# All sixteen modulation rows of the first feed-forward made by TensorE in four column tiles of 32

## The chip, the cores and the metric

The kernel runs on one core of one Trainium2 chip. The time is device time in microseconds (us), the median of three runs. The core has a matrix engine (TensorE, PE in the profile, whose weight loads are listed as PEld), a vector engine (VectorE, DVE), a scalar engine (ScalarE, ACT), GpSimd (POOL) and a queue engine that issues transfers (SyncE, SP). Each of them runs its own instructions in the order in which they stand.

## The reference

One layer of a streaming encoder over 1024 tokens of width 1024, in float32. A conditioning vector makes nine modulation vectors of 1024 numbers, and the first two of them (shift `sh1` and scale `sc1`) enter the input of the first feed-forward:

```python
c_act = jax.nn.silu(c)
mod = c_act @ w_mod[l] + b_mod[l]
sh1, sc1, gt1, sh2, sc2, gt2, sh3, sc3, gt3 = jnp.split(mod, N_MOD, axis=-1)
u = modulate(rmsnorm(h, ffn1_norm_g[l]), sh1, sc1)      # u * (1 + sc1) + sh1
h = h + 0.5 * gt1[:, None, :] * swiglu(u, ffn1_w_gate[l], ffn1_w_up[l], ffn1_w_down[l])
```

Latent attention beside an RWKV-7 mixer, a second feed-forward and a last norm follow; they are not touched.

## The kernel before, in words

Activations lie transposed: 128 of the 1024 features on the partitions, tokens along the free dimension, so that an activation is eight tiles d = 0..7 for each half a = 0, 1 of 512 tokens. The first feed-forward begins with `up_plain`, which makes two blocks of the hidden layer without the seven-product scheme of the later ones. For half 0, and then for half 1, it multiplies the eight input tiles by two gate and two up blocks into four accumulators; each product is three matmuls on a high and a low part (`mm3`, L66). That is 96 matmuls of 512 columns for each half, 12 for each input tile. An input tile is ready when it has been normalized (`norm_raw`, L315 to L319: even d by VectorE and ScalarE, odd d by GpSimd and ScalarE), which needs the modulation numbers of its d, and when it has been split (`split`, L59 on ScalarE, then L60 on VectorE). The first low-part matmul of a tile waits for L60.

A modulation row is 128 numbers of one vector v for one d. For the first feed-forward there are sixteen: v = 0 (shift) and v = 1 (scale), d = 0..7. Those of d = 0 and 1 are made by `mod_first` on TensorE: per row eight matmuls, each with one column of the conditioning vector as weights, into one partition of a PSUM tile; a copy by ScalarE (L155), two small matmuls that turn the rows into columns (L158), and an addition of the bias by VectorE (L161). Those of d = 2..7 are made by `mod_one` on VectorE: a product with the spread vector `cact`, summed along the free dimension (L138, with a read of the accumulator), and an addition (L141). `cact` is made by `spread_c` (L117, L118). It is also used later by `mod_steps` for the other seven vectors.

Half 1 needs the sums of squares of its tokens first (`root(1)`: squares L202 on ScalarE, additions L206 on VectorE, eight small matmuls L214, square root L252, reciprocal L253, and `spread` with L224, one matmul L228 and a copy L229). The squares (`nsq`) and the copied rows (`row`) take their room in turn from the same four slots `fs[8:]`, in the order in which the program asks for them. The PSUM tiles called `norm` take turns in banks 6 and 7.

The program is written once in this order, but the scheduler of the tile framework moves each engine's instructions by its own estimate of when they can run. What stands where in the built program is shown with the change.

Of the kernel before, what the change touches and what calls it, by code (L numbers as in the profile page):

```python
# [22 lines left out]
P = 128  # L23
D = 1024
S = 1024
HB = 512
ND = D // P
# [48 lines left out]
def ps(k, name):  # L76
    b = next(k.bank[name])
    return k.psum.tile([P, HB], F32, name="ps_" + name, tag=f"bank{b}", bufs=1)


def tmp(k, name, n=HB, dt=F32):

    pool, tag, size = next(k.spare if n == HB else k.wide)
    return pool.tile([P, size], dt, name=name, tag=tag)[:, :n]
# [44 lines left out]
def mod_loads(k, v, d):  # L129
    w = tmp(k, "wmod", D)  # L130
    k.nc.sync.dma_start(out=w, in_=k.I["w_mod"][v * ND + d])
    return w


def mod_one(k, v, d, w):

    m = k.mod[:, v, d : d + 1]
    k.nc.vector.scalar_tensor_tensor(  # L138
        out=w, in0=w, scalar=1.0, in1=k.cact, op0=ALU.mult, op1=ALU.mult, accum_out=m
    )  # L140
    k.nc.vector.tensor_tensor(out=m, in0=m, in1=k.bmod[:, v * ND + d : v * ND + d + 1], op=ALU.add)  # L141


def mod_first(k, d, w):

    nc = k.nc
    t = ps(k, "norm")
    for v in range(2):
        for i in range(ND):
            nc.tensor.matmul(  # L150
                t[0:1, v * P : (v + 1) * P], lhsT=k.ccol[:, i : i + 1], rhs=w[v][:, i * P : (i + 1) * P],
                start=i == 0, stop=i == ND - 1,
            )
    row = tmp(k, "row")[0:1, : 2 * P]
    nc.scalar.copy(out=row, in_=t[0:1, : 2 * P])  # L155
    t = ps(k, "norm")[:, :2]
    for v in range(2):
        nc.tensor.matmul(  # L158
            t[:, v : v + 1], lhsT=row[:, v * P : (v + 1) * P], rhs=k.ones[0:1, 0:1], start=True, stop=True
        )  # L160
    nc.vector.tensor_tensor(  # L161
        out=k.mod[:, :2, d], in0=t, in1=k.bmod[:, : 2 * ND].rearrange("p (v d) -> p v d", d=ND)[:, :, d], op=ALU.add
    )
# [593 lines left out]
def scratch(k, pool):  # L757
    d = lambda name, *shape: [pool.tile([P, *shape], F32, name=f"{name}{a}") for a in range(2)]
    k.hD = d("hD", ND, HB)
    k.hidD = [pool.tile([P, D], F32, name=f"hidD{i}") for i in range(NF)]  # L760
    k.sinD = d("sinD", HB)
    k.cosD = d("cosD", HB)
    k.arD = d("arD", NJ, 8, P)
    k.m3D = d("m3D", 8, 8, 2, L)
    k.akD = d("akD", 8, 4, L)
    k.vD = d("vD", 4, NJ, P)
    k.ybD = d("ybD", NJ, HB)
    k.oD = d("oD", NH, HB)
    k.boD = d("boD", NJ, HB)
    k.lgD = d("lgD", NJ, HB)  # L770
    k.xD, k.fD = (pool.tile([8 * NCH, L, L], F32, name=n) for n in ("xD", "fD"))
    k.tD = pool.tile([8 * NCH, HL, HL], F32, name="tD")
# [767 lines left out]
def setup(ctx, k, tc, I, out):  # L1540
    k.nc = nc = tc.nc
    k.tc = tc
    k.I = I
    k.out = out
    k.const = ctx.enter_context(tc.tile_pool(name="const", bufs=1, side="left"))
    k.dram = ctx.enter_context(tc.tile_pool(name="dram", bufs=1, space=DRAM))
    ct = lambda name, *shape, dt=F32: k.const.tile([P, *shape], dt, name=name)
    k.ident = ct("ident", P)
    make_identity(nc, k.ident)
    k.ones = ct("ones", P)  # L1550
    nc.gpsimd.memset(k.ones, 1.0)
    for name, value in (("eps", EPS), ("halfpi", math.pi / 2)):
        setattr(k, name, ct(name, 1))
        nc.gpsimd.memset(getattr(k, name), value)
    k.bd = ct("bd", P)
    nc.gpsimd.memset(k.bd, 0.0)
    nc.gpsimd.memset(k.bd[0:64, 0:64], 1.0)
    nc.gpsimd.memset(k.bd[64:128, 64:128], 1.0)
    k.cst = ct("cst", 2 + P)
    nc.scalar.dma_start(out=k.cst, in_=I["cst"])  # L1560
    k.wmask = k.cst[:, 2:]
    k.mod = ct("mod", 9, ND)
    k.WL = ct("WL", NJ, NCH)
    k.oss = ct("oss", 8)
    k.qs = ct("qs", 2, 8)
    k.gs = {n: ct("gs_" + n, ND) for n in ("ffn1_norm_g", "mix_norm_g", "ffn2_norm_g")}
    scratch(k, k.dram)
# [19 lines left out]
def tile_layer(ctx, tc, I, out):  # L1587
    k = Ctx()
    setup(ctx, k, tc, I, out)
    nc = k.nc  # L1590
# [10 lines left out]
    with pool_("ffn1") as pool:  # L1601
# [15 lines left out]
        early = 2  # L1617
        slices = {}

        def load_mods(ds):  # L1620
            for d in ds:
                for v in (1, 0):
                    if d < early:
                        w = slices[v, d] = tmp(k, "wmod", D)
                        nc.sync.dma_start(out=w.rearrange("p (i q) -> p i q", q=P), in_=I["w_mod_in"][v * ND + d])
                    else:
                        slices[v, d] = mod_loads(k, v, d)

        def mods(d):
            if d < early:  # L1630
                mod_first(k, d, [slices[v, d] for v in range(2)])
            else:
                for v in (1, 0):
                    mod_one(k, v, d, slices[v, d])
            gain(k, "ffn1_norm_g", 1, slice(d, d + 1))

        load_mods(range(early))
# [29 lines left out]
        x = []  # L1667
# [96 lines left out]
    with pool_("inv", "left") as ip, pool_("chain") as pool:  # L1764
# [8 lines left out]
        for p in range(NP2):  # L1773
            o = ops.pop(0)
            even, odd, norm, gate = outputs(k, pool, o)
# [46 lines left out]
    x = []  # L1822
# [101 lines left out]
```

## Time and profile before

| | |
|---|---|
| median of three runs | 2100.34 us (2097.65 to 2102.45) |
| the profiled execution | 2099.98 us, of which its span is 2098.1 us |
| TensorE busy | 2023.0 us, 96% of the span |
| VectorE busy | 1508.9 us, 72% |
| ScalarE busy | 926.8 us, 44% |
| TensorE busy in the first 100 us | 81.06 us |

The span runs from the first instruction to the last. Busy times of different engines overlap. A busy matrix engine can still be held up, since the ends of its matmuls are modelled; how many matmuls run in a stretch tells more.

### The profile page before, as it was taken

The page shows a single profiled execution, that of the slowest core. Times are in us where ns is not written, and L with a number is a line of the kernel's source. Part 1 is how long each engine was busy: PE and PEld are TensorE (multiplying, and loading weights), DVE is VectorE, ACT ScalarE, POOL GpSimd, SP SyncE. Part 2 cuts the span into 40 slices and gives each one's busy share as a digit, 9 for nine tenths or more (in the row PEclk, how much of TensorE's full clock was granted, in tenths as well). Part 3 has the DMA queues.
Part 4 walks back from the last instruction along what each step waited for, and adds up shares of the span by engine and source line. Part 5 has one row for each costly group of instructions (what it writes and reads, how often), then busy time and mean ns, then how long its engine had stood idle before and what let it go on. Part 6 is the DMA issues. An engine that isn't in the chain of part 4 may idle for free.

```text
span 2098.1 us, 28595 instructions
## 1 busy us (share of the span) xinstructions
PE 2023.0 (96%) x10624; PEld 1636.3 (78%) x10624; DVE 1508.9 (72%) x2710; ACT 926.8 (44%) x1600; POOL 232.3 (11%) x250
## 2 busy tenths in 40 slices
PE   6999999999999999898979999999999999999998
PEld 4788878887888776676868888787888888878887
DVE  6999896569996567697565666567556556599975
ACT  5643333344433466644344444455333333453433
POOL 1100000000000244332133222111000000000001
PEclk8999999999999999999999999999999999999999
DMA  8277742235333124545336773750222212353322
GB/s 333 83 246 232 241 141 89 82 126 186 116 103 108 66 60 123 153 136 146 89 84 172 201 181 110 239 178 36 84 77 90 87 65 97 103 192 107 105 70 81
DMA packets 182220, 273.75 MB, mean 130 GB/s; under 512 B 77120, under 2 KB 113344, under 8 KB 182080
## 3 DMA queue, kind: packets, MB, share of 16 engines
q1 hardware_dynamic: 180368, 268.62, 40.6%
q0 software_dynamic: 1280, 3.15, 0.5%
q8 instruction: 84, 1.38, 0.3%
q14 instruction: 56, 0.46, 0.1%
q10 hardware_dynamic: 432, 0.15, 0.0%
HBM read 202.66 MB, written 66.58 MB: 128 GB/s over the span
## 4 chain that ended last, share of the span: by engine, by line
PE 72%; DVE 13%; DMA 7%; issue 4%; ACT 3%; POOL 1%; SPq 0%; DVEq 0%; ACTq 0%; POOLq 0%
PE ps_w L66 32%; PE ps_dn L66 21%; PE ps_in L66 5%; PE ps_wo L66 3%; DMA wmod<-w_mod 2%; DVE pair L60 2%; PE ps_ov L1235 2%; PE ps_z L1422 2%; DVE wmod L138 2%; PE ps_s L66 1%; DVE Tpr L1324 1%; DVE T L1328 1%; PE ps_y L1449 1%; PE ps_y L1448 1%; PE ps_pt L1227 1%
## 5 line engine op out<-in xcount | busy, mean ns | idle before, releaser
L66 PE MATMUL ps_w<-pair 128*128 128x512 f32 x3744 | 876.6, 395 | 14.1 <-ACT pair L59 9.9
L66 PEld LDWEIGHTS ps_w<-pair 128*128 128x128 f32 x3744 | 704.4, 188 | 183.6 <-ACT pair L59 10.6
L60 DVE TENSOR_TENSOR pair<-raw,pair 128x512 fp32r<-128x512 f32 x256 | 177.0, 699 | 106.1 <-ACT pair L59 106.0
L59 ACT CAST pair<-raw 128x512 fp32r<-128x512 f32 x256 | 154.9, 621 | 222.3 <-PE ps_w L66 174.6
L66 PE MATMUL ps_in<-pair,win 128*128 128x512 f32 x960 | 245.1, 409 | 2.9 <-ACT pair L280 2.2
L66 PE MATMUL ps_dn<-pair 128*128 128x512 f32 x1008 | 236.6, 393 | 2.4 <-DVE part L608 1.5
L66 PEld LDWEIGHTS ps_dn<-pair 128*128 128x128 f32 x1008 | 188.9, 188 | 47.3 <-DVE part L608 2.4
L66 PEld LDWEIGHTS ps_in<-pair,win 128*128 128x128 f32 x960 | 182.5, 193 | 52.2 <-issue 9.1
L66 PE MATMUL ps_dn<-pair,dh 128*128 128x512 f32 (+1 forms) x704 | 204.2, 375 | 0.0
L66 PEld LDWEIGHTS ps_dn<-pair,dh 128*128 128x128 f32 x704 | 128.1, 188 | 25.8 <-issue 0.7
L388 ACT COPY part<-ps_w 128x512 f32<-128x512 f32 x120 | 70.0, 585 | 163.3 <-PE ps_w L66 152.4
L66 PE MATMUL ps_dn<-pair,dl 128*128 128x512 f32 (+1 forms) x352 | 131.2, 375 | 0.0
L551 DVE SCALAR_TENSOR_TENSOR h<-ps_dn,mod,h 128x512 f32<-128x512 f32 (+1 forms) x128 | 90.3, 712 | 37.6 <-PE ps_dn L66 37.2
L59 ACT CAST pair<-hraw 128x512 fp32r<-128x512 f32 x124 | 73.3, 620 | 68.8 <-DMA hraw<-hidD 29.7
L206 POOL TENSOR_TENSOR nacc<-nacc,nsq 128x512 f32<-128x512 f32 x12 | 17.7, 1476 | 665.9 <-ACT nsq L202 665.9
L138 DVE SCALAR_TENSOR_TENSOR wmod<-wmod,cact 128x1024 f32<-128x1024 f32 x68 | 82.8, 1220 | 9.8 <-DMA wmod<-w_mod 9.8
L486 DVE TENSOR_TENSOR t<-ps_w,part 128x512 f32<-128x512 f32 x80 | 54.5, 687 | 45.4 <-PE ps_w L66 26.8
L60 DVE TENSOR_TENSOR pair<-hraw,pair 128x512 fp32r<-128x512 f32 x124 | 82.8, 684 | 4.8 <-ACT pair L59 4.6
L66 PE MATMUL ps_wo<-pair,woh 128*128 128x512 f32 x256 | 79.9, 393 | 0.0
L699 POOL TENSOR_TENSOR h<-h,nr 128x256 f32<-128x256 f32 (+1 forms) x6 | 5.4, 916 | 649.1 <-ACT nr L229 649.1
L66 PEld LDWEIGHTS ps_dn<-pair,dl 128*128 128x128 f32 x352 | 66.3, 188 | 12.8 <-issue 0.2
L481 DVE TENSOR_TENSOR c<-ps_w,part 128x512 f32<-128x512 f32 x80 | 53.3, 685 | 29.1 <-PE ps_w L66 23.5
(348 smaller groups left out, 3002.5 us busy)
## 6 DMA issues: line engine op xcount, KB each, us to landing
wmod<-w_mod SPq DMA_DIRECT2D x68, 512.0 KB, 4.4
raw<-ffn_w_gate SPq DMA_DIRECT2D x44, 512.0 KB, 3.7
raw<-ffn_w_up SPq DMA_DIRECT2D x44, 512.0 KB, 4.5
hidD<-c SPq DMA_DIRECT2D x44, 512.0 KB, 2.9
hraw<-hidD SPq DMA_DIRECT2D x44, 512.0 KB, 3.4
draw<-ffn_w_down SPq DMA_DIRECT2D x40, 512.0 KB, 3.5
h<-x SPq DMA_DIRECT2D x32, 256.0 KB, 4.5
hD<-h SPq DMA_DIRECT2D x32, 256.0 KB, 2.0
```

The costliest lines, as they stand in the source:

```text
L59: k.nc.scalar.copy(out=hi, in_=src)
L60: k.nc.vector.tensor_tensor(out=lo, in0=src, in1=hi.bitcast(F32), op=ALU.subtract)
L66: k.nc.tensor.matmul(out, lhsT=x, rhs=y, start=start, stop=stop, skip_group_check=onto)
L138: k.nc.vector.scalar_tensor_tensor(out=w, in0=w, scalar=1.0, in1=k.cact, op0=ALU.mult, op1=ALU.mult, accum_out=m)
L388: nc.scalar.copy(out=t, in_=x)
L481: nc.vector.tensor_tensor(out=c[i][:, j], in0=x, in1=y, op=ALU.add)
L486: nc.vector.tensor_tensor(out=t, in0=x, in1=y, op=ALU.add)
L551: nc.vector.scalar_tensor_tensor(out=y, in0=x, scalar=gt[:, d : d + 1], in1=y, op0=ALU.mult, op1=ALU.add)
L1227: nc.tensor.transpose(tp[:, q : q + P], pr[:, s0 + q : s0 + q + P], k.ident)
L1235: nc.tensor.matmul(x.po[:, cols], lhsT=pt[:, b * P : (b + 1) * P], rhs=k.v[b][:, cols], start=b == 0, stop=b == x.i)
L1324: nc.vector.tensor_tensor(out=v, in0=T[:, t, 0:m][:, None, :].broadcast_to([P, n, m]), in1=xp[:, t, m:][:, :, None].broadcast_to([P, n, m] ...
L1422: nc.tensor.matmul(t[u, h], lhsT=lhs[:, h], rhs=rhs[:, h], start=True, stop=True)
```

## The change

`mod_first` now makes the rows of all eight d, and `mod_one` is left to the later vectors. The eight matmuls of a row no longer add up in one partition: matmul x goes to column tile q = x // 2, where its one weight column, repeated 32 times, fills 32 partitions of the PSUM tile. Each of the four tiles then holds the sum of two products. ScalarE copies 128 x 256 numbers (before: 1 x 256), and the turning matmul has 128 rows and a vector `quarters` that is one at partitions 0, 32, 64 and 96 and zero elsewhere, which adds up the four partial sums. The weights of all sixteen rows come from `w_mod_in`, whose layout suits TensorE; the size of each load is the same 512 KB.

```diff
 def mod_first(k, d, w):
...
+    t = ps(k, "norm")[:, : 2 * P]
+    n = ND // 4
     for v in range(2):
-        for i in range(ND):
-            nc.tensor.matmul(
-                t[0:1, v * P : (v + 1) * P], lhsT=k.ccol[:, i : i + 1], rhs=w[v][:, i * P : (i + 1) * P],
-                start=i == 0, stop=i == ND - 1,
-            )
-    row = tmp(k, "row")[0:1, : 2 * P]
-    nc.scalar.copy(out=row, in_=t[0:1, : 2 * P])
+        for i in range(n):
+            for q in range(4):
+                x = q * n + i
+                nc.tensor.matmul(
+                    t[32 * q : 32 * q + 32, v * P : (v + 1) * P], lhsT=k.ccol[:, x : x + 1].broadcast_to([P, 32]),
+                    rhs=w[v][:, x * P : (x + 1) * P], start=i == 0, stop=i == n - 1,
+                )
+    row = tmp(k, "row")[:, : 2 * P]
+    nc.scalar.copy(out=row, in_=t)
     t = ps(k, "norm")[:, :2]
     for v in range(2):
-        nc.tensor.matmul(
-            t[:, v : v + 1], lhsT=row[:, v * P : (v + 1) * P], rhs=k.ones[0:1, 0:1], start=True, stop=True
-        )
+        nc.tensor.matmul(t[:, v : v + 1], lhsT=row[:, v * P : (v + 1) * P], rhs=k.quarters, start=True, stop=True)
...
+    k.quarters = ct("quarters", 1)
+    nc.gpsimd.memset(k.quarters, 0.0)
+    for q in range(0, P, 32):
+        nc.gpsimd.memset(k.quarters[q : q + 1], 1.0)
...
         def load_mods(ds):
             for d in ds:
                 for v in (1, 0):
-                    if d < early:
-                        w = slices[v, d] = tmp(k, "wmod", D)
-                        nc.sync.dma_start(out=w.rearrange("p (i q) -> p i q", q=P), in_=I["w_mod_in"][v * ND + d])
-                    else:
-                        slices[v, d] = mod_loads(k, v, d)
+                    w = slices[v, d] = tmp(k, "wmod", D)
+                    nc.sync.dma_start(out=w.rearrange("p (i q) -> p i q", q=P), in_=I["w_mod_in"][v * ND + d])
         def mods(d):
-            if d < early:
-                mod_first(k, d, [slices[v, d] for v in range(2)])
-            else:
-                for v in (1, 0):
-                    mod_one(k, v, d, slices[v, d])
+            mod_first(k, d, [slices[v, d] for v in range(2)])
             gain(k, "ffn1_norm_g", 1, slice(d, d + 1))
```

Lines of the changed kernel stand up to six higher in `mod_first` and two higher after it, so L154, L159, L162 and L163 are what L150, L155, L158 and L161 were, and L204, L216, L230 and L255 are L202, L214, L228 and L253.

**TensorE, from the rows of d = 1 on.** `ps_w` with four different numbers are the four accumulators of half 0; `ps_norm` from `wmod` are modulation rows. Before:

```order
L150 MATMUL ps_norm<-wmod,ccol 1x128 x16
L158 MATMUL ps_norm<-ones,row 128x1 x2
L66 MATMUL ps_w_466<-pair 128x512
L66 MATMUL ps_w_491<-pair 128x512
L66 MATMUL ps_w_519<-pair 128x512
L66 MATMUL ps_w_544<-pair 128x512
L66 MATMUL ps_w_466<-pair 128x512 x2
L66 MATMUL ps_w_491<-pair 128x512 x2
L66 MATMUL ps_w_519<-pair 128x512 x2
L66 MATMUL ps_w_544<-pair 128x512 x2
```

After:

```order
L154 MATMUL ps_norm<-wmod,ccol 32x128 x16
L162 MATMUL ps_norm<-quarters,row 128x1 x2
L66 MATMUL ps_w_586<-pair 128x512
L66 MATMUL ps_w_611<-pair 128x512
L66 MATMUL ps_w_639<-pair 128x512
L66 MATMUL ps_w_664<-pair 128x512
L154 MATMUL ps_norm<-wmod,ccol 32x128 x16
L66 MATMUL ps_w_586<-pair 128x512 x5
L66 MATMUL ps_w_611<-pair 128x512 x5
L66 MATMUL ps_w_639<-pair 128x512 x5
L66 MATMUL ps_w_664<-pair 128x512 x5
L162 MATMUL ps_norm<-quarters,row 128x1 x2
```

The rows of d = 2 stand behind the first four matmuls of half 0, and their turning matmuls behind twenty more; the rows of d = 3 to 7 follow in the same way among the matmuls of half 0, the turning matmuls of d = 3 and d = 5 right behind the matmuls of their own rows.

**ScalarE, up to the first splits of half 0.** `h_0_146` and `h_0_152` are the tile that holds d = 0 and 1 of half 0. Before:

```order
L155 COPY row<-ps_norm 1x256
L118 ACT_TABLE_LOAD
L118 ACTIVATE cact<-cact 128x1024
L319 ACTIVATE h_0_146<-h_0_146,mod 128x512
L59 CAST pair<-h_0_146 128x512
L316 ACTIVATE h_0_146<-h_0_146,mod,gs_ffn_norm_g 128x512
L59 CAST pair<-h_0_146 128x512
```

After:

```order
L159 COPY row<-ps_norm 128x256
L59 CAST pair<-raw 128x512 x6
L321 ACTIVATE h_0_152<-h_0_152,mod 128x512
L318 ACTIVATE h_0_152<-h_0_152,mod,gs_ffn_norm_g 128x512
L118 ACT_TABLE_LOAD
L118 ACTIVATE cact<-cact 128x1024
L59 CAST pair<-h_0_152 128x512 x2
```

The making of `cact` has moved from ahead of the first tile's normalization to between that and its split.

**TensorE, at the sums of squares of half 1.** `ps_w_466` and its three partners are accumulators of half 0; `ps_w_691` and its partners are those of half 1. Before, the last two of the eight sums and what follows:

```order
L214 MATMUL ps_norm<-ones,nacc 128x1
L214 MATMUL ps_norm<-ones,nsq 128x1
L66 MATMUL ps_w_466<-pair 128x512
L66 MATMUL ps_w_491<-pair 128x512
L66 MATMUL ps_w_519<-pair 128x512
L66 MATMUL ps_w_544<-pair 128x512
L66 MATMUL ps_w_466<-pair 128x512 x3
```

After, the same two:

```order
L216 MATMUL ps_norm<-ones,nacc 128x1
L216 MATMUL ps_norm<-ones,nsq 128x1
L230 MATMUL ps_norm<-nr,ones 128x512
L66 MATMUL ps_w_691<-pair 128x512
L66 MATMUL ps_w_716<-pair 128x512
L66 MATMUL ps_w_744<-pair 128x512
L66 MATMUL ps_w_769<-pair 128x512
```

The sums and the spreading matmul stood in the middle of half 0; now they stand behind its last matmul and ahead of the first of half 1. From there on, the order on TensorE is the same in both but for a few places further down where neighbours have changed places.

## Rows read from the trace of the kernel before

**Rows 1.** The page: busy time by engine, share of the span, instructions.

```profile
PE 2023.0 (96%) x10624; PEld 1636.3 (78%) x10624; DVE 1508.9 (72%) x2710; ACT 926.8 (44%) x1600; POOL 232.3 (11%) x250
```

**Rows 2.** Windows: stretch, length, busy (instructions) by engine, clock, DMA share, GB/s.

```profile
0.00:100.00 100.00, 81.06 (x342) 59.45 (x343) 80.31 (x140) 59.81 (x97) 13.43 (x20) 0.93 0.54 204
100.00:200.00 100.00, 100.00 (x433) 81.08 (x433) 93.45 (x186) 38.23 (x68) 0.00 (x0) 1.00 0.74 246
```

**Rows 3.** Timeline of TensorE: start, length, what, count of records, [idle before <-releaser].

```profile
15.02 3.65 PE L150 MATMUL ps_norm<-wmod,ccol 128*1 128x128 f32 x32
19.18 0.60 PE L158 MATMUL ps_norm<-ones,row 1*128 1x1 f32 x4 [0.51 <-ACT row L155]
...
30.56 11.75 PE L66 MATMUL ps_w<-pair 128*128 128x512 f32 x40 [6.09 <-ACT pair L59]
...
44.42 0.28 PE L214 MATMUL ps_norm<-ones,nacc 128*128 128x1 f32 x2
...
45.90 0.36 PE L214 MATMUL ps_norm<-ones,nsq 128*128 128x1 f32 x2
50.07 8.14 PE L66 MATMUL ps_w<-pair 128*128 128x512 f32 x24 [3.81 <-ACT pair L59]
58.05 1.02 PE L228 MATMUL ps_norm<-nr,ones 128*128 128x512 f32 x2
58.51 6.52 PE L66 MATMUL ps_w<-pair 128*128 128x512 f32 x26
67.13 8.20 PE L66 MATMUL ps_w<-pair 128*128 128x512 f32 x34 [2.10 <-DVE pair L60]
```

**Rows 4.** The rows of d = 2 to 7 on VectorE: one tile's instructions, ns min/median/max.

```profile
L138 DVE SCALAR_TENSOR_TENSOR wmod<-wmod,cact x12: 1207/1218/1220, 30.3 to 53.5; 128x1024 f32<-128x1024 f32 x12
L138 DVE DVE_READ_ACCUMULATOR wmod<-wmod,cact x12: 75/82/84, 31.4 to 54.7; 128x1 f32 x12
```

**Rows 5.** Timeline of TensorE at the column tiles of the mixer.

```profile
1114.27 0.28 PE L1202 MATMUL ps_s<-kr,qr 128*128 128x256 f32 x1
1114.39 0.28 PE L1203 MATMUL ps_s<-kr,qr 128*128 128x256 f32 x1
1114.60 0.44 PE L1352 MATMUL ps_t<-T,w 128*32 128x32 f32 x8
```

**Rows 6.** Windows of line L1352 on TensorE: within one column tile, then where two meet.

```profile
1112.80:1112.90 0.10, 0.10 (x6) 1.00 0.97 220
1113.09:1113.19 0.10, 0.10 (x11) 1.00 0.90 195
```

**Rows 7.** Timeline of ScalarE around the first splits and the square root.

```profile
23.84 1.28 ACT L118 ACT_TABLE_LOAD   x1
25.13 1.06 ACT L118 ACTIVATE cact<-cact 128x1024 f32<-128x1024 f32 x1
...
31.68 0.82 ACT L316 ACTIVATE h<-h,mod,gs_ffn_norm_g 128x512 f32<-128x512 f32 x1 [1.18 <-DVE gs_ffn_norm_g L184]
...
42.13 1.28 ACT L252 ACT_TABLE_LOAD   x1
46.30 0.26 ACT L252 ACTIVATE rt<-ps_norm,eps 128x4 f32<-128x4 f32 x1 [2.89 <-PE ps_norm L214]
```

**Rows 8.** Windows of five microseconds: busy by engine, then granted clock.

```profile
30.00:35.00 5.00, 4.44 (x11) 3.40 (x12) 5.00 (x13) 2.48 (x4) 0.00 (x0) 0.53 1.04 405
35.00:40.00 5.00, 5.00 (x24) 4.10 (x23) 4.63 (x12) 4.01 (x8) 0.00 (x0) 1.00 1.02 409
```

**Rows 9.** Timeline of VectorE from the spread of half 1 to its first split.

```profile
59.30 0.68 DVE L374 TENSOR_TENSOR raw<-raw 128x512 f32<-128x512 f32 x1
59.90 2.71 DVE L318 SCALAR_TENSOR_TENSOR h<-h,gs_ffn_norm_g,ps_norm 128x512 f32<-128x512 f32 x4
62.53 3.94 DVE L353 TENSOR_TENSOR h<-h,h 128x512 f32<-128x512 f32 x3
66.40 1.28 DVE L60 TENSOR_TENSOR pair<-h,pair 128x512 fp32r<-128x512 f32 x2
```

More of the change, by code (lines that the diff above doesn't have):

```diff
@@ L146, in mod_first @@
     nc = k.nc
-    t = ps(k, "norm")
+    t = ps(k, "norm")[:, : 2 * P]
+    n = ND // 4
     for v in range(2):
-        for i in range(ND):
-            nc.tensor.matmul(
-                t[0:1, v * P : (v + 1) * P], lhsT=k.ccol[:, i : i + 1], rhs=w[v][:, i * P : (i + 1) * P],
-                start=i == 0, stop=i == ND - 1,
-            )
-    row = tmp(k, "row")[0:1, : 2 * P]
-    nc.scalar.copy(out=row, in_=t[0:1, : 2 * P])
+        for i in range(n):
[7 more added lines that the diff above has]
+    nc.scalar.copy(out=row, in_=t)
     t = ps(k, "norm")[:, :2]
     for v in range(2):
-        nc.tensor.matmul(
-            t[:, v : v + 1], lhsT=row[:, v * P : (v + 1) * P], rhs=k.ones[0:1, 0:1], start=True, stop=True
-        )
+        nc.tensor.matmul(t[:, v : v + 1], lhsT=row[:, v * P : (v + 1) * P], rhs=k.quarters, start=True, stop=True)
     nc.vector.tensor_tensor(
```

## The prediction

> **What bounds the kernel now.** I read the page first. TensorE is busy for 2023.0 of 2098.1 us [rows 1], so time is lost or gained where TensorE stands idle, and the windows say where: in the first 100 us it is busy for 81.06 us and runs 342 matmuls, in the next 100 us it is busy throughout and runs 433 [rows 2], one every 0.231 us. That is its own pace, for back to back it does 34 in 8.20 us, 0.241 each [rows 3]. Whatever the change does, it does at the start. If the dense stretch begins later, everything behind it begins later by as much: VectorE has slack there, but TensorE has none to give back, and its order is the same.
>
> The timeline of TensorE [rows 3] is the view to read next. It makes the rows of d = 0 and 1 from 15.02 to 24.47, then waits 6.09 us for the first split of half 0. Half 0 runs from 30.56 to 65.03 (58.51 + 6.52) and holds the eight sums of squares of half 1 (44.42 to 46.26), a wait of 3.81 us ahead of 50.07, and the spreading matmul at 58.05. Then 2.10 us are lost, and half 1 runs on from 67.13. In half 0 it is VectorE that is late, with twelve products of 1218 ns and twelve reads of 82 ns [rows 4], 15.6 us in all. These the change takes away. The question is whether TensorE can use that.
>
> **What the rows cost on TensorE.** A matmul in float32 is two records, and the 16 matmuls of one d take 3.65 us for 32 records now, 0.114 us each with the next one starting as the last is done [rows 3]. In four column tiles they could overlap. The trace has a nearest case in the mixer, with tiles of 32 columns: inside one tile 6 records touch a stretch of 0.10 us, and where the work passes from one tile to another it is 11, at the same clock [rows 6]. So two column tiles do run at once. But the two records of one matmul go to the same tile and stand next to each other, so the second has to wait for the first, and only neighbouring matmuls overlap. I take half, 1.83 us for one d. The bounds are a quarter (0.91 us, all four tiles at once) and the whole (3.65 us, no overlap).
>
> The Trainium skill, "TensorE: Matmul & The Clock Gate", section on packing small matmuls, says that a pack of tiles takes one matmul's length and some 4 ns for each further tile; by that the 16 matmuls would take about 0.9 us (an estimate), and the result would be that of the first rival below.
>
> Going from whole-array matmuls to column tiles costs something too. L1203 starts 0.12 us after L1202, and L1352, the first in column tiles, 0.21 us after L1203 [rows 5]. So 0.1 us for one switch, 0.2 us for going there and back.
>
> The skill's "TensorEngine Tiling (Array Packing)", Key Properties, says that changing the tiling mode drains TensorE, which speaks against rows strewn among other matmuls; the trace agrees, with 0.1 us.
>
> The turning matmuls take 0.60 us for one d [rows 3], with 128 rows as with one, since they are still four records on a 128-column weight. Between the rows and the turning lies ScalarE's copy, and TensorE waited 0.51 us for it [rows 3]; where other matmuls stand between, that is hidden, where none do (d = 3 and 5), it is not.
>
> **Step 1, the first matmul of half 0.** ScalarE now has an activation (0.82 us), a table load (1.28 us) and the spread conditioning vector (1.06 us) between the first normalized tile and its split [rows 7], 3.16 us in all. Before, the load and the vector lay in ScalarE's idle time, and that was their cover. VectorE comes to the normalization about a microsecond earlier, since fewer weight splits stand ahead. Bounds 0 and 3.2 us later; I take 2, so 32.6. The rows of d = 2 to 7 cannot use the long idle time before, for they stand behind this matmul, and TensorE does not pass it.
>
> **Step 2, half 0.** 96 matmuls at 0.241 us are 23.1 us. After the idle time the granted clock was 0.53 of full speed from 30 to 35 us, 11 matmuls where the next 5 us had 24 [rows 8], a loss of about 2.3 us; it comes again, on the first matmuls and the rows of d = 2. Six d at 1.83 + 0.60 + 0.2 us are 15.8 us, and two waits of 0.51 us make 1.0. The sum is 42.2 us, all on TensorE with hardly a wait for others left, because VectorE is ahead now. Half 0 ends at 74.8, 9.8 us later than at 65.03. Nothing hides the rows: TensorE is the engine that the rest waits for.
>
> **Step 3, from half 0 to half 1.** Before, the sums, the root and the spread of half 1 were made inside half 0. Now `row` and `nsq` share four slots, and the program asks for the rows of d = 4 to 7 before the squares of half 1; so the squares of half 1 wait until those rows are turned, the last of them late in half 0, and the scheduler put the sums behind half 0. The chain is bare: the sums take 1.8 us (44.42 to 46.26 [rows 3]), beside two activations of the accumulators on ScalarE (about 0.6 us each, estimated by the length of its other 512-column work) and a table load of 1.28 us, then the root of 0.26 us [rows 7], the reciprocal, and two VectorE operations of 0.68 us [rows 9]. From 74.8 that is 0.2 + 1.2 + 1.28 + 0.26 + 0.2 + 1.4 and small handovers, so the spread begins at about 79.5. From the spread to the first matmul that needs a low part it was 9.1 us (58.05 to 67.13 [rows 3]): the matmul, four normalizations (2.71 us), three differences (3.94 us) and the split [rows 9]. Some work of half 0 that stood between is gone from there, say 0.7 us. So 79.5 + 8.4 = 87.9, 20.8 us after 67.13. By then four matmuls of half 1 are done in place of two: 0.5 us back.
>
> Four more edits cost nothing: five small memsets on GpSimd, which is idle until about 20 us; 12 loads that take the same bytes from another tensor in the same place of the queue; six larger copies on ScalarE, which waits for TensorE there; six additions in place of twelve on VectorE. If the cover of the copies were gone, they would cost what the 0.51 us above says.
>
> **The sum**: 20.8 - 0.5 = 20.3 us, on 2099.98 us for the profiled execution (span 2098.1, and 1.9 around it), which is 0.4 us under the median of the runs: 2120.5 us for the median.
>
> **Rivals.**
> (1) All four tiles at once: six times 0.92 us less, 2115. For it: the array does overlap two tiles [rows 6]. Against: two records of a matmul on one tile.
> (2) No overlap: six times 1.82 us more, and the rows of d = 2 at the lower clock, 2132. For it: the pieces of one row go into one PSUM bank, and the case of rows 6 is a tile boundary and not a steady stream.
> (3) The other side, faster: VectorE's 15.6 us leave half 0, and TensorE makes the rows in time that it only waited. Its waits from 24.47 to 67.13 are 6.09 + 3.81 + 2.10 us, and with the lower clock after the second wait some 2 us more. If the rows went ahead of half 0's first matmul and cost no more than a quarter, the last three would vanish: about 8 us, 2092. It decides at the place of the rows and of the sums: with both inside waits, faster; with both on TensorE's chain, slower. The built order speaks against both.
> (4) No change: the rows fill the waits of half 0 just so and the chain to half 1 is hidden, 2100. The same order speaks against it.
> (5) The clock falls again, as the rows leave most of the array idle: each 5 us at the lower clock costs 2.3 us [rows 8], over half 0 some 20 us more, 2140.
>
> **How the numbers follow.** Forecast 0.54 (2116 to 2126 with the bounds of step 1 and of small waits), (1) 0.18, (2) 0.14, (3) 0.05, (4) 0.04, (5) 0.05. The range from 2112 to 2133 holds the forecast, (1) and (2), 0.86. A measurement of this kernel tells 0.2%, about 4 us, from no change. Faster 0.05, the same 0.04, slower 0.91.
>
> **What would show it.** In the profile after: 16 matmuls of one d in 1.8 us, and a gap of 0.2 us around them; first matmul of half 0 at 32 to 33 us; half 0 until about 75; one gap of some 8 us, broken by the spread, ahead of half 1, which runs on from about 88; from 100 us on the same count of matmuls in each stretch as before, 20 us later. I am wrong if TensorE has no gap between the halves, or if the rows run ahead of 30 us, or if the stretches behind 100 us differ by more than the shift.

## The result, and the profile after

The changed kernel takes 2114.88 us (median of five, 2111.34 to 2117.77) where the kernel before takes 2100.34; the ratio is 1.0065, 95% interval 1.0052 to 1.0077. So it is slower by 14.5 us. The forecast was 2120.5 with a range from 2112 to 2133; the number that came out is that of rival (1). The profiled execution has a span of 2112.2 us, 14.1 over before.

The timeline of TensorE after (start, length, engine, line, output<-input, count of records, [idle before <-releaser]); it answers to [rows 3]:

```profile
13.53 1.08 PE L154 MATMUL ps_norm<-wmod,ccol 128*32 128x128 f32 x32
16.07 0.58 PE L162 MATMUL ps_norm<-quarters,row 128*128 128x1 f32 x4 [1.46 <-ACT row L159]
...
30.92 2.08 PE L66 MATMUL ps_w<-pair 128*128 128x512 f32 x4 [10.71 <-ACT pair L59]
32.92 1.94 PE L154 MATMUL ps_norm<-wmod,ccol 128*32 128x128 f32 x32
34.79 5.08 PE L66 MATMUL ps_w<-pair 128*128 128x512 f32 x20
39.71 0.50 PE L162 MATMUL ps_norm<-quarters,row 128*128 128x1 f32 x4
40.14 1.08 PE L154 MATMUL ps_norm<-wmod,ccol 128*32 128x128 f32 x32
...
44.12 1.08 PE L154 MATMUL ps_norm<-wmod,ccol 128*32 128x128 f32 x32
45.13 4.85 PE L66 MATMUL ps_w<-pair 128*128 128x512 f32 x20
...
61.52 5.75 PE L66 MATMUL ps_w<-pair 128*128 128x512 f32 x24
67.11 0.28 PE L216 MATMUL ps_norm<-ones,nacc 128*128 128x1 f32 x2
...
70.92 2.04 PE L230 MATMUL ps_norm<-nr,ones 128*128 128x512 f32 x2 [1.98 <-DVE nr L226]
77.01 2.08 PE L66 MATMUL ps_w<-pair 128*128 128x512 f32 x4 [4.04 <-ACT pair L59]
80.89 19.37 PE L66 MATMUL ps_w<-pair 128*128 128x512 f32 x72 [1.81 <-DVE pair L60]
```

Three things are to be seen. The 16 matmuls of one d take 1.08 us, not 3.65. Half 0 runs from 30.92 to 67.27 (61.52 + 5.75), 36.35 us where it was 34.47 before. And between 67.27 and 80.89 TensorE does eight small sums, one spread and four matmuls: a gap of 13.6 us where before 2.1 us were lost. The dense stretch begins 13.8 us later, and 11.5 of these are the gap.

The windows after, to be held against [rows 2] (stretch, length, busy and instructions of PE, PEld, DVE, ACT, POOL, granted clock, DMA share, GB/s):

```profile
0.00:100.00 100.00, 71.24 (x494) 52.69 (x495) 56.31 (x89) 55.18 (x91) 13.78 (x25) 0.83 0.46 176
100.00:200.00 100.00, 100.00 (x437) 81.73 (x436) 93.85 (x183) 38.54 (x68) 0.00 (x0) 1.00 0.72 238
80.00:85.00 5.00, 4.11 (x10) 3.24 (x11) 5.00 (x10) 5.00 (x10) 0.00 (x0) 0.50 0.00 0
```

In the first 100 us TensorE is busy for 71.24 us, 9.8 less. From 80 to 85 the granted clock is 0.50, the lower of the two levels (1.2 GHz), after a gap in which the engine did little, and ten matmuls run where 24 ran in five microseconds at the full clock [rows 8]. And from 100 us on there are 437 matmuls in 100 us where there were 433: the dense work itself is 1% faster than before. Nothing in the forecast said that.

How much of the lead of the kernel before is left further down can be read at two places in the mixer, the first low-rank matmul (L898 before, L900 after) and the first attention matmul (L1202, L1204). TensorE reaches them at 760.53 and 1107.19 before, at 769.87 and 1118.82 after. So of the 13.8 us only 9.3 are left when the mixer begins, 11.6 when attention begins, and 14.1 at the end.

### The profile page after: what moved, and what is told of

It reads as the page before. It is cut to its first block, busy times and chain, and to the rows that moved or that the text cites. A ratio compares the mean times of both kernels' runs of the same rounds, so it can differ in the third digit from the quotient of the medians.

```text
span 2112.2 us, 29041 instructions
## 1 busy us (share of the span) xinstructions
PE 2026.6 (96%) x10840; PEld 1643.2 (78%) x10840; DVE 1496.3 (71%) x2680; ACT 928.4 (44%) x1606; POOL 233.6 (11%) x255
## 4 chain that ended last, share of the span: by engine, by line
PE 71%; DVE 15%; DMA 6%; issue 4%; ACT 3%; POOL 1%; SPq 0%; DVEq 0%; POOLq 0%; ACTq 0%
PE ps_w L66 31%; PE ps_dn L66 20%; PE ps_in L66 5%; PE ps_wo L66 3%; DVE pair L60 2%; PE ps_ov L1237 2%; PE ps_z L1424 2%; DMA wmod<-w_mod 1%; PE ps_s L66 1%; DVE wmod L138 1%; DVE Tpr L1326 1%; DVE T L1330 1%; PE ps_y L1451 1%; PE ps_t L1354 1%; PE ps_y L1450 1%
## 5 line engine op out<-in xcount | busy, mean ns | idle before, releaser
L138 DVE SCALAR_TENSOR_TENSOR wmod<-wmod,cact 128x1024 f32<-128x1024 f32 x56 | 68.0, 1218 | 8.2 <-DMA wmod<-w_mod 8.2
```

The costliest lines, as they stand in the source:

```text
L138: k.nc.vector.scalar_tensor_tensor(out=w, in0=w, scalar=1.0, in1=k.cact, op0=ALU.mult, op1=ALU.mult, accum_out=m)
```

## The experiments

The table holds what the timelines of TensorE say of each kernel in its own profiled execution; "first" is the first matmul of half 0, "dense" where the uninterrupted stretch of half 1 begins, "mixer" the time from the first low-rank to the first attention matmul. Ratios are to the kernel before, run beside it on the same chip, where its median was 2098.63 to 2101.60 us.

| kernel | median us | ratio (95%) | first | dense | mixer |
|---|---|---|---|---|---|
| before | 2100.34 | 1 | 30.56 | 67.13 | 346.7 |
| after | 2114.88 | 1.0065 (1.0052 to 1.0077) | 30.92 | 80.89 | 349.0 |
| held slots, rows as before | 2098.86 | 0.9999 (0.9988 to 1.0010) | 30.41 | 76.56 | 336.4 |
| after, rows in the wide ring | 2102.36 | 1.0009 (1.0000 to 1.0019) | 30.94 | 77.52 | 338.1 |
| after, no column tiles | 2121.19 | 1.0097 (1.0081 to 1.0114) | 29.61 | 95.35 | 337.8 |
| after, rows twice | 2117.92 | 1.0086 (1.0068 to 1.0103) | 31.45 | 88.17 | 347.8 |
| after, early spread vector | 2110.14 | 1.0053 (1.0039 to 1.0067) | 23.95 | 79.33 | 349.6 |
| the same in the wide ring | 2114.37 | 1.0061 (1.0046 to 1.0076) | 24.61 | 80.75 | 347.5 |
| wide ring, spread in half 0 | 2108.48 | 1.0043 (1.0029 to 1.0056) | 32.43 | 76.07 | 346.6 |
| before, two rows tiled | 2103.83 | 1.0016 (1.0005 to 1.0027) | 31.73 | 69.35 | 346.8 |
| before, three rows, wide ring | 2089.05 | 0.9945 (0.9933 to 0.9957) | 27.54 | 65.54 | 339.9 |
| before, three rows, shared slots | 2083.95 | 0.9929 (0.9915 to 0.9942) | 23.80 | 63.60 | 336.3 |
| before, four rows, wide ring | 2089.34 | 0.9956 (0.9943 to 0.9969) | 29.27 | 64.66 | 334.8 |
| before, vector alone | 2097.90 | 0.9985 (0.9975 to 0.9995) | 30.02 | 66.62 | 347.1 |

The column "mixer" has two groups, 346.6 to 349.6 and 334.8 to 339.9, and the group does not follow the number of rows on TensorE: with all eight d there it is 349.0 us in the changed kernel and 338.1 with the wide ring. Without these groups the totals mislead; "The order of the mixer" tells of them.

### The hold of the slots alone

```diff
             else:
                 for v in (1, 0):
                     mod_one(k, v, d, slices[v, d])
+                row = tmp(k, "row")[:, :1]
+                nc.scalar.copy(out=row, in_=k.mod[:, 0, d : d + 1])
```

(This is in the kernel before. In the trace the copy is L1636.)

> The kernel before, with its rows of d = 2 to 7 on VectorE as they were, plus one small copy for each d on ScalarE of a finished column into a tile of the four slots that the squares of half 1 use. The copy's result is read by nobody. So the squares of half 1 have to wait for the columns of d = 4 to 7 as in the changed kernel, and nothing else of the change is there. Theory: the sums, the root and the spread slip behind half 0, and a gap of 5 to 10 us opens: 2105 to 2110. Rival (rows on TensorE make the loss): 2100 to 2102.

By the total (2098.86 us) it has no effect, and both ranges are missed. At the start the sums and the spread slip behind half 0, as the theory says, and the gap is wider than its 5 to 10 us. ScalarE, then TensorE, of this kernel:

```profile
42.22 0.19 ACT L1636 COPY row<-mod 128x1 f32<-128x1 f32 x1 [3.44 <-DVE mod L141]
42.45 0.63 ACT L202 ACTIVATE nsq<-h 128x512 f32<-128x512 f32 x1
```

```profile
52.61 10.32 PE L66 MATMUL ps_w<-pair 128*128 128x512 f32 x32 [1.67 <-DVE pair L60]
62.76 0.28 PE L214 MATMUL ps_norm<-ones,nacc 128*128 128x1 f32 x2
...
66.58 2.05 PE L228 MATMUL ps_norm<-nr,ones 128*128 128x512 f32 x2 [1.98 <-DVE nr L224]
72.67 2.08 PE L66 MATMUL ps_w<-pair 128*128 128x512 f32 x4 [4.04 <-ACT pair L59]
76.56 23.65 PE L66 MATMUL ps_w<-pair 128*128 128x512 f32 x89 [1.81 <-DVE pair L60]
```

The squares of half 1 now follow the small copies, the sums stand behind half 0, and the gap is 13.6 us (62.93 to 76.56), the same as after, with every row of d = 2 to 7 still on VectorE. The dense stretch begins 9.4 us later than before. So the hold of the four slots is enough to open the gap of the changed kernel, and no row on TensorE is needed for it; whether the gap goes when the hold goes is asked below (the wide ring). What the total hides is that the mixer of this kernel takes 336.4 us and not 346.7.

### The order of the mixer

The scheduler moves instructions by its own estimate of times, and an edit at the start can shift that. In one group of kernels the mixer has the order that it has in before and after. In the other (in a variant where the mixer takes 339.9) the head sums `kk` (L915 before, L917 after) and what follows stand later among the input projections. The group of these matmuls on TensorE (busy us, mean ns, then idle time before them and its releaser), first of before, then of the run with the spread in half 0, then of the run with the wide ring:

```profile
L915 PE MATMUL ps_kk<-kk,bd 128*128 128x512 f32 x16 | 10.7, 758 | 6.7 <-ACT kk L913 6.7
```

```profile
L917 PE MATMUL ps_kk<-kk,bd 128*128 128x512 f32 x16 | 11.4, 805 | 8.0 <-ACT kk L915 8.0
```

```profile
L917 PE MATMUL ps_kk<-kk,bd 128*128 128x512 f32 x16 | 8.8, 631 | 0.5 <-ACT kk L915 0.5
```

In the first order TensorE comes to `kk` before ScalarE has it and waits up to 4.9 us at once, after which it goes on at the lower clock (0.50 granted from 900.6 to 903.1 us after). One such place after, and the same place in the run with the wide ring:

```profile
900.63 2.07 PE L917 MATMUL ps_kk<-kk,bd 128*128 128x512 f32 x2 [4.85 <-ACT kk L915]
901.72 1.41 PE L66 MATMUL ps_in<-pair,win 128*128 128x512 f32 x1
```

```profile
888.86 1.12 PE L917 MATMUL ps_kk<-kk,bd 128*128 128x512 f32 x2 [0.52 <-ACT kk L915]
```

The windows of the whole stretch, of the run with the spread in half 0 and of that with the wide ring, say it in sum: 346.5 us with a mean clock of 0.96, 338.1 us with 0.98, for the same work.

```profile
766.90:1113.40 346.50, 315.48 (x1603) 243.66 (x1603) 247.71 (x379) 178.95 (x263) 113.73 (x134) 0.96 0.42 116
```

```profile
765.60:1103.70 338.10, 310.39 (x1604) 240.51 (x1604) 251.14 (x380) 176.84 (x262) 115.98 (x135) 0.98 0.43 119
```

These two enter the mixer within 1.3 us of each other, so a late start is not what makes the difference. An edit at the start that flips the mixer's order gets some 7 to 15 us there that it has not earned. Some 4 of these are lost again: from the first attention matmul to the end the kernels with the short mixer take 996.0 to 998.5 us, the others 990.7 to 995.4 (999.6 in one). Why was not followed. Totals may be compared only within one group, and starts by "dense".

### The wide ring

```diff
-    row = tmp(k, "row")[:, : 2 * P]
+    row = tmp(k, "row", D)[:, : 2 * P]
```

> The changed kernel with one edit: the rows are copied into a tile of the wide ring, so that they no longer share four slots with the squares of half 1. Same work, same result. Theory (the bare chain of sums, root, spread and normalization between the halves makes the loss): the squares of half 1 run on ScalarE early again (before 45 us), the eight sums go into half 0, and only the spread, the normalization and the split stand behind it; the gap between the halves (13.6 us of TensorE in the changed kernel) falls to about 9 us, and the time from 2115 to between 2106 and 2112. Rival (the rows' time on TensorE inside half 0 makes the loss): half 0 stays as long, the gap is not what counts, 2113 to 2116.

The total fell to 2102.36 us, by more than the theory allowed, and the theory does not get that credit: the mixer is 11 us shorter (338.1 for 349.0), of which 3.9 are lost again behind it. At the start the sums are back in half 0 and the gap shrinks as expected; the dense stretch begins 3.4 us earlier.

```profile
59.60 0.36 PE L216 MATMUL ps_norm<-ones,nacc 128*128 128x1 f32 x2
...
61.39 7.35 PE L66 MATMUL ps_w<-pair 128*128 128x512 f32 x24
68.58 1.02 PE L230 MATMUL ps_norm<-nr,ones 128*128 128x512 f32 x2
73.64 2.08 PE L66 MATMUL ps_w<-pair 128*128 128x512 f32 x4 [4.04 <-ACT pair L59]
77.52 22.80 PE L66 MATMUL ps_w<-pair 128*128 128x512 f32 x86 [1.80 <-DVE pair L60]
```

The sums and the root are now inside half 0, which gets 1.4 us longer (30.94 to 68.74), and the gap shrinks to 8.8 us. What is left of it is the spread, four normalizations, three differences and the split, and these are still bare. So the hold is not the whole cause. From the first matmul of half 0 to the dense stretch it is 36.6 us before, 46.2 with the hold alone, 46.6 here, with the rows on TensorE and no hold, and 50.0 in the changed kernel: each by itself costs some 10 us, both together 13.4.

### The spread inside half 0

```diff
-            x.append(normed(1, root(1)))
+            with tc.high_priority(offset=1500):
+                r1 = root(1)
+            x.append(normed(1, r1))
```

(On top of the wide ring.)

> The run with the rows in the wide ring, plus one edit: the sums and the root of half 1 are given a higher priority, so that the spread of half 1 stands eight matmuls after the last row, inside half 0, and not behind half 0's last matmul. Its mixer keeps the order of the kernels before and after, so its total is compared with that of the changed kernel, and its start with that of the run with the wide ring. Theory (the chain from the spread to the first split of half 1 is bare only because of its place): the dense stretch begins at 72 to 75 for 77.52 there and 80.89 in the changed kernel; 2106 to 2110. Rival (VectorE and ScalarE are busy with half 0 until then, so the place of the spread alone moves nothing): dense from 76 to 78, 2111 to 2114.

```profile
66.48 1.02 PE L230 MATMUL ps_norm<-nr,ones 128*128 128x512 f32 x2
66.94 3.33 PE L66 MATMUL ps_w<-pair 128*128 128x512 f32 x12
73.00 2.08 PE L66 MATMUL ps_w<-pair 128*128 128x512 f32 x4 [2.73 <-ACT pair L59]
76.07 24.23 PE L66 MATMUL ps_w<-pair 128*128 128x512 f32 x98 [0.99 <-DVE pair L60]
```

As it stands, the 76.07 lies in the rival's range and the total of 2108.48 in the theory's. But the profiled execution reached half 0 1.5 us later than the run with the wide ring (32.43 for 30.94), so the distance from there to the dense stretch is compared: 43.6 us here, 46.6 with the wide ring. The gap is 5.8 us, and the total is 0.2% under that of the changed kernel, with a mixer of the same group; the two intervals still touch. So moving the chain back into half 0, the sums by the wide ring and the spread by this edit, is worth 6.3 of the 13.4 us by which the changed kernel's distance is longer. Of the rest, 3.4 us are that half 0 itself is longer (37.8 for 34.5), with the rows on TensorE, and 3.7 the gap (5.8 for 2.1): the spread still stands only twelve matmuls (3.3 us) ahead of the end of half 0 where 24 stood before.

### The price of the rows

```diff
-    for v in range(2):
+    for v in (0, 1, 0, 1):
         for i in range(n):
```

> The changed kernel with the matmuls of each row done twice (the second pass starts afresh and gives the same numbers). It measures the price of the rows by itself: 16 more matmuls for each d, 1.08 us by the trace of the changed kernel. Theory: rows stand on TensorE's chain in half 0, six times 1.08 us and some at the lower clock: 6 to 8 us more, 2121 to 2123. Rival (only the gap between the halves counts, the rows fill waits): 2115 to 2117.

```profile
36.87 1.95 PE L154 MATMUL ps_norm<-wmod,ccol 128*32 128x128 f32 x64
```

From the first matmul of half 0 to the dense stretch it is 56.7 us, 6.7 more than the 50.0 of the changed kernel, which is in the 6 to 8 of the theory; the 32 matmuls took 1.95 us, 0.87 more than 16, six times which is 5.2. So what a row takes on TensorE does stand on the path. The total rose by 3.0 us only, to 2117.92, between the two ranges, and its interval overlaps that of the changed kernel. In the profiled execution 3.5 us are gone again between the dense stretch and the mixer (685.4 us for 689.0) and 1.1 in the mixer; why was not followed.

```diff
-        for i in range(n):
-            for q in range(4):
...
+        for i in range(ND):
+            nc.tensor.matmul(
+                t[0:1, v * P : (v + 1) * P], lhsT=k.ccol[:, i : i + 1], rhs=w[v][:, i * P : (i + 1) * P],
```

(All eight d stay on TensorE, but as d = 0 and 1 were made before.)

> The changed kernel with one edit: all eight d stay on TensorE, but each row is made by sixteen matmuls into one partition, as the kernel before does for d = 0 and 1. Same result. Here the 16 matmuls of one d take 3.65 us in place of 1.08 us. Theory: half 0 is on TensorE's chain, so six times 2.57 us, 15 us, less what waits of half 0 absorb: 2124 to 2130. Rival (rows fill waits that TensorE has anyway, and only the chain between the halves counts): 2115 to 2119.

From the first matmul of half 0 to the dense stretch it is 65.7 us, 15.8 more than in the changed kernel, and six times 2.57 (3.65 - 1.08) is 15.4: the whole price again. The total, 2121.19, is below the 2124 of the theory because this kernel has the shorter mixer (337.8 for 349.0, of which 3.8 are lost again behind it). The two runs together say that in half 0 of the changed kernel TensorE's time for a row is paid in full.

### The spread vector

```diff
         r0 = root(0)
+        spread_c(k, pool)
...
-            spread_c(k, pool)
```

> The changed kernel with one edit: the spread conditioning vector (a table load and an activation on ScalarE, 2.34 us) is asked for directly behind the root of half 0, ahead of the first normalization. The order of the mixer is that of the changed kernel. If that vector holds up the first matmul of half 0, that one comes 2 to 7 us earlier than at 30.92. Theory (TensorE's own work in half 0 and the bare chain behind it set the end): half 0 ends 3 to 4 us earlier, 2110 to 2112. Rival (half 0 is held by the rows and their handovers wherever it begins): 2114 to 2116.

```profile
27.93 5.89 PE L66 MATMUL ps_w<-pair 128*128 128x512 f32 x14 [2.76 <-DVE pair L60]
```

The first matmul of half 0 came 7 us earlier, at 23.95, but half 0 ended only 0.9 us earlier (66.37 for 67.27), where the theory had 3 to 4, and the dense stretch began 1.6 earlier. Half 0 soon waits 2.76 us for the next split and goes on at the lower clock (0.57 granted from 28 to 34 us). So `cact` ahead of the first split costs at most these 1.6 us. That the total, 2110.14, lies in the theory's range is luck: of the 4.6 us by which the profiled execution is shorter, the start gives 1.6, and the intervals of the two ratios overlap.

> The run before this one with the rows also in the wide ring, away from the squares' slots; the order of the mixer stays that of the changed kernel, so that this time the slots are seen without a change elsewhere. Theory: 3 to 4 us less than the run before this one, as the dense stretch of the first run with the wide ring began 3.4 us earlier (77.52 for 80.89): 2106 to 2109. Rival (the whole gain of that run, 12.5 us, came from the slots): 2098 to 2102.

This is a miss, above both ranges. With both edits the dense stretch begins 1.4 us later than with the early vector alone, not 3.4 earlier; 0.7 of that is a later begin of half 0 (24.61). The eight squares of half 1, free of their slots, now stand on ScalarE ahead of the split of the next input tile, the last three of them behind that tile's row, and TensorE waits for the split and goes on at the lower clock (0.50 granted):

```profile
39.51 1.15 ACT L204 ACTIVATE nsq<-h 128x512 f32<-128x512 f32 x2
41.17 0.62 ACT L204 ACTIVATE nsq<-h 128x512 f32<-128x512 f32 x1
41.69 0.60 ACT L59 CAST pair<-h 128x512 fp32r<-128x512 f32 x1
```

```profile
42.35 5.49 PE L66 MATMUL ps_w<-pair 128*128 128x512 f32 x12 [2.08 <-ACT pair L59]
```

Twelve matmuls took 5.49 us, 0.46 each, twice the usual. In the first run with the wide ring the squares fell behind the first splits, where ScalarE was idle. So freeing the slots helps or hurts by where the squares land, and the theory that the hold as such costs the time holds only for the kernel in which it was tested. The total rose by more than the start explains: behind the first attention matmul this execution takes 999.6 us where that of the early vector alone takes 990.7.

### The column tiles alone, and what they are good for

```diff
-    t = ps(k, "norm")
+    t = ps(k, "norm")[:, : 2 * P]
...
-                t[0:1, v * P : (v + 1) * P], lhsT=k.ccol[:, i : i + 1], rhs=w[v][:, i * P : (i + 1) * P],
+                    t[32 * q : 32 * q + 32, v * P : (v + 1) * P], lhsT=k.ccol[:, x : x + 1].broadcast_to([P, 32]),
```

(In the kernel before: `mod_first` and the vector `quarters` are those of the changed kernel, `load_mods` and `mods` are not touched, so d = 2 to 7 stay with VectorE.)

> The kernel before, with one edit: the rows of d = 0 and 1, which TensorE makes there already, are made in four column tiles; d = 2 to 7 stay on VectorE. So the start is nearly that of the kernel before (dense from 67 to 68). The scheduler gives this program the mixer's order of the runs with the wide ring and with the held slots, not that of the kernels before and after. Theory (that order of the mixer, not the start, gave those runs some 9 to 12 us between the mixer's first and its first attention matmul): 2088 to 2092. Rival (the order is worth nothing, and what those runs won had to do with their late start): 2098 to 2102.

The condition of this expectation did not hold. The program that ran has the mixer's order of the kernel before (346.8 us), so the run says nothing on that order. It does say that faster rows of d = 0 and 1 are worth nothing alone: TensorE is done with them some 3 us sooner (21.02 for 24.47), and the first matmul of half 0 still comes at 31.73, because the scheduler now puts `cact` ahead of the first split, as in the changed kernel.

```diff
-        early = 2
+        early = 3
```

(On top of the run before this one. In two further runs the rows are in the wide ring and the spread vector comes early, with `early` 3 and 4. In the second of the three texts that follow, "the run before this one" is the run with two rows tiled.)

> The kernel before with the column tiles for d = 0, 1 and 2 (d = 3 to 7 on VectorE); rows in the squares' four slots and the spread conditioning vector where it was. The start is nearly that of the kernel before (dense from 65 to 69). The program has the mixer's order of the runs that took 336 to 338 us from the first low-rank matmul (line 898 of before) to the first attention matmul (line 1202 of before), where the kernels before and after take 347 and 349. Theory (that order is worth some 9 us wherever it stands): 2089 to 2093. Rival (it is worth something only behind a late start): 2098 to 2101.

> The kernel before with the column tiles for d = 0, 1 and 2 alone (d = 3 to 7 on VectorE), the rows in the wide ring, the spread conditioning vector asked for behind the root of half 0. The mixer's order is again the other one. The row of d = 2 now stands ahead of half 0 in TensorE's order, in its idle time. Theory: first matmul of half 0 before 28 us, dense from 63 to 67, 0 to 3 us less than the run before this one: 2085 to 2091, below both kernels. Rival (what TensorE gains at the start it loses in waits for VectorE in half 0): as the run before this one or 2 us more.

> The run with three rows on TensorE, the wide ring and the early spread vector, with a fourth row (d = 3) moved to TensorE. Four rows stand ahead of half 0. It asks how many rows TensorE's idle time ahead of half 0 holds. Theory: the fourth row still fits, half 0 begins about 1 to 3 us later and waits less for VectorE inside; dense from 63 to 66, 2085 to 2089. Rival (the fourth row delays half 0 by its length and the waits inside are not VectorE's products any more): 2089 to 2093.

All three beat both kernels. With the wide ring, three rows (2089.05) fall in the range of their theory and four (2089.34) just above theirs, in the rival's. The best is the plainest, 2083.95 us, below the range of its theory and 14.7 us (0.7%) under the kernel before by the medians on the same chip. Its start:

```profile
18.37 1.65 PE L154 MATMUL ps_norm<-wmod,ccol 128*32 128x128 f32 x32 [0.55 <-ACT row L159]
...
23.80 0.79 PE L66 MATMUL ps_w<-pair 128*128 128x512 f32 x1 [0.54 <-ACT pair L59]
...
63.60 36.66 PE L66 MATMUL ps_w<-pair 128*128 128x512 f32 x153 [3.41 <-DVE pair L60]
```

The row of d = 2 stands ahead of half 0, in TensorE's idle time. The dense stretch begins 3.5 us earlier than before. From there to the mixer it takes 686.7 us for 693.4, and the next experiment tells where most of these 6.7 us are from. The mixer's order gives 10.4, and 5.6 are lost again behind it. So of the 15.1 us by which the profiled execution is shorter, the start can claim 3.5, and not all of it is the row of d = 2: in this kernel the making of `cact` has moved behind the first splits (its table load is at 28.90 where it was at 23.84 before), so that the first matmul of half 0 comes at 23.80. With four rows ahead of half 0 (64.66) there was no further gain.

### The vector alone

```diff
+    k.quarters = ct("quarters", 1)
+    nc.gpsimd.memset(k.quarters, 0.0)
+    for q in range(0, P, 32):
+        nc.gpsimd.memset(k.quarters[q : q + 1], 1.0)
```

(On top of the kernel before; nothing reads it.)

> The kernel before plus the vector that the changed kernel adds (one column in the constants' pool and its five memsets on GpSimd), read by nobody. The order on TensorE, VectorE and ScalarE is that of the kernel before. In the changed kernel and in most other runs that have this vector, TensorE did 437 matmuls in a full 100 us of the first feed-forward, in the kernel before and in the run with held slots, which lack it, 433 or 434; behind 1400 us all did 433. Theory (the vector shifts the tiles' addresses, and the faster pace comes with that): 436 or 437 matmuls from 100 to 200 us, 4 to 6 us less in the feed-forward, 2093 to 2097. Rival (the pace comes with the rows in column tiles, or with which weights are loaded where): 433, 2099 to 2102.

```profile
100.00:200.00 100.00, 100.00 (x437) 81.81 (x436) 93.79 (x187) 38.18 (x68) 0.00 (x0) 1.00 0.74 244
...
1500.00:1600.00 100.00, 100.00 (x434) 80.80 (x433) 56.26 (x87) 36.07 (x63) 0.00 (x0) 1.00 0.26 89
```

The pace is 437 with the vector and nothing else of the change, so the rows have no part in it. TensorE begins half 1's dense stretch 0.5 us earlier than before and the mixer 5.8 us earlier (754.7 for 760.53). The total is 0.15% lower, 3.7 us by the medians on the same chip, and at 2097.90 between the two ranges. The order of instructions on the three engines is the same. What differs is a column in the constants' pool, for which the tiles behind it must make room, and five memsets on GpSimd, which are done by 2.2 us. That a shift of addresses speeds the matmuls up is the likely reading, but it is not shown, and which tile would matter was not tried. Nor does the vector always pay: the run with two rows tiled has it and reaches 437 only from 300 us on, since TensorE waits now and then before that (430 matmuls from 100 to 200, 421 from 200 to 300).

## Why the prediction was right in its range, and where its steps failed

The range held the time, and the mechanism held: the rows stand on TensorE's path inside half 0, the chain between the halves is bare, and the time is lost in the first 100 us. The likeliest case was 5.6 us too high, and its own bounds, 2116 to 2126, missed the time by 1.1 us.

**The cost of a row was mis-sized.** Taken was 1.83 us of 0.91 to 3.65; it was 1.08. The ground for it, that the two records of a float32 matmul go to one tile and so only neighbouring matmuls overlap, does not show. Records of L154 after in three windows of 0.11 us, then of L150 before in one:

```profile
13.60:13.71 0.11, 0.11 (x8) 0.11 (x12) 1.00 1.00 410
13.82:13.93 0.11, 0.11 (x16) 0.11 (x8) 1.00 1.09 447
14.04:14.15 0.11, 0.11 (x16) 0.11 (x8) 1.00 1.10 447
```

```profile
15.20:15.31 0.11, 0.11 (x3) 0.08 (x2) 1.00 0.92 373
```

Up to sixteen records touch a stretch of 0.11 us where three did. (So the prediction's reading that a record starts as the last is done was wrong too: a record before is listed with 0.27 us, and the next starts after 0.11.) In the trace after, four records start 7 ns apart, one behind the other, and the next four 0.11 us after the first ones, the pace of single records before: four tiles run at a time, and the 16 matmuls pass at 0.067 us each. The Trainium skill, "TensorE: Matmul & The Clock Gate", section "Part 3: Packing small matmuls", would have given about 0.9 us (an estimate), and the trace agrees within 0.2, with 7 ns from one tile to the next where the page says some 4. The switch of the tiling mode (0.1) and the turning (0.60) were taken too long as well: L162 is followed 0.43 us later by the next row (39.71, 40.14), and a row 1.01 us later by matmuls of half 0 (44.12, 45.13). In sum a d takes 1.44 us of TensorE, not 2.63, and six of them 7.1 us less.

**Step 1** gave 32.6 for the first matmul of half 0; it was 30.92. ScalarE's 3.16 us did move ahead of the split, but the rows and the first normalization came earlier by nearly as much, and the run with the early vector shows that little hung on this.

**Step 2** gave 42.2 us for half 0; it was 36.35. The 7.1 us above explain more than that, and 1.3 came back in longer waits for copies and splits.

**Step 3** gave 13.1 us from the end of half 0 to the dense stretch; it was 13.6. That it came so near is in part luck: the spread began 3.65 us behind half 0 where 4.7 was taken, and from there to the dense stretch it was 9.97 us where 8.4 was taken (the spreading matmul alone took 2.04 us for 1.02). The reason given, the four slots, opens the same gap by itself; but without it, in the wide ring, 8.8 us of the gap stay.

By these three steps the dense stretch was forecast for 87.9 and began at 80.89, 7.0 us earlier: 1.7 + 5.9 - 0.5.

**What the sum left out.** Behind the gap the first matmuls of the dense stretch run at the lower clock (ten from 80 to 85), which no step had. The claim that four edits cost nothing was wrong for the vector, which gives back 3.7 us; and so was the claim that each stretch behind 100 us has the same count of matmuls (437 for 433), which had been named as a sign of being wrong. Between the start of the mixer and the end 4.8 us come on top (9.3 to 14.1), 2.3 up to the first attention matmul and 2.4 behind it; they were not traced to a cause.

**The rivals.** (1) was right in its mechanism, four tiles at once, and in its number; the faster pace between 100 and 760 us (13.8 to 9.3) and the loss behind it (9.3 to 14.1), of which it knew nothing, cancel. That it hit the time is luck to that extent, and so is that the 13.8 us at the start and the 14.1 at the end are so near to each other. (2) is excluded by the row's 1.08 us; the kernel without column tiles, where they do take 3.65, begins its dense stretch at 95.35. (3) decides where it was said to, at the place of the rows: with one more row ahead of half 0 (and `cact` behind the first splits) the dense stretch begins 3.5 us earlier than before. (4) did not come about. Nor did (5): from 40 to 67 us, with five of the six rows strewn among the matmuls of half 0, the granted clock was 1.00, and it had been 1.00 for the rows of d = 0 and 1 before, too.

## What to carry to other kernels

Work that was moved onto the bounding engine cost its full time where it stood among that engine's own work (0.87 us more for each row put the dense stretch back by more than six times that), and nothing that shows where it stood ahead of a wait: with one row more ahead of half 0 the dense stretch came 3.5 us earlier, in part by a ScalarE order that changed with it. Ask of every tile that shares a ring which later work the ring now holds back: here four slots by themselves made a chain bare that had been hidden. Freeing them in the changed kernel won less (3.4 us) than holding them cost in the kernel before (9.4), for with the rows on TensorE the spread stayed behind half 0. And where a scheduler orders the program, compare stage by stage, since an edit at the start changed the length of a stage 700 us later by 10 us.

## What was not expected of the hardware

Four column tiles of 32 columns with float32 matmuls of 128 columns overlap almost fully: 3.65 us became 1.08 (1.95 for twice the work). And one unread column of constants went with a 600 us stretch of matmuls that is 1% faster (437 for 433 in 100 us).
